# An encoder layer in split fp32: seven-product projection pairs ahead of the mixers, and new fill between the mixers' steps

## The chip, the cores and the metric

The kernel runs on one core of one Trainium2 chip. The metric is the device time of one execution in microseconds (us). Engines are named as the profile names them: PE is the matrix engine, DVE, ACT and POOL work on vectors, and SP issues transfers. Line numbers such as L633 are those of the kernel before, unless the text says that they are of the kernel after.

## The reference

One layer of a bidirectional encoder on x, 1024 tokens by 1024 features, in fp32:

```python
u = x @ W_in                            # rq, rk, rv, rg (512 each), aq (512), ak, av (128 each)
y_ret = retention(rq, rk / 8, rv)       # 8 heads of 64, forward and backward, chunks of 128
y_ret = groupnorm(y_ret) * silu(rg)
y_att = windowed_attention(aq, ak, av)  # 8 query heads, 2 key heads, +-128 tokens, sink logit
h = LN1(ALPHA * x + concat(y_ret, y_att) @ W_out)
f = (silu(h @ W_g) * (h @ W_u)) @ W_d + sigmoid(h @ W_pg) * (p @ W_pe)
out = LN2(ALPHA * h + f)                # ALPHA = 2 ** 0.25, W_g and W_u are 1024 x 2816
```

## The kernel before

**Arithmetic.** Every fp32 operand of a large matmul is split into a high and a low part (`split`, L73 on ACT for the high part and L74 on DVE for the low one). One product of two such operands is three PE matmuls (`mm3`, L77 to L79): high by high, high by low, low by high. Each has a stationary block of 128x128 and 512 moving columns. In this text "a product" is such a triple and "a matmul" is one of its three.

**Stages in order.**

1. *First f-tiles* (L132 to L180). A column tile of 128 features of `u` is an f-tile. Four f-tiles (the first attention query tile, ak, rk of pair 0, rq of pair 0) are accumulated in all eight banks of PSUM while x streams in. The split x stays in four buffers named H.
2. *Mixers* (up to L600). Four pairs of heads, each with a retention (`Retention`) and an attention (`Attention`). Their steps are short matmuls with DVE, ACT and POOL work between them, so the program interleaves them with *fill*: steps of one product of the rest of the input projection, taken from `queue`. PE's order is written out by hand here (`manual_schedule` for PE); the other engines' orders come from a scheduler. `run(steps, total)` spreads `total` fill steps evenly over the places marked `F`. The fill is 288 steps: 14 f-tiles of 16 steps, and rv, which `proj_rv` makes in token-major form in 64 steps. Attention 0 runs in 16 + 64 of them, retention 0 in 48, then three iterations (retention i with attention i) in 48 each, and 16 remain for the end. In the names below, K is `keys` (transposes of rk at L363, times a decay on DVE at L366), C is `kv` (L377 on PE, L381 on DVE), Q is the scores of the retention, Y its output, N its norm, and X the transposes that turn the normed result (L455 on PE, L456 on ACT).
3. *Output projection* (L568 to L690). The eight mixer results are split (yT) and multiplied by w_out: 384 matmuls. Tokens come in eight tiles of 128 (t = 0 to 7), each in two halves of 512 columns. Phase 1 does t = 0 to 3 for all eight k-tiles in eight banks (192 matmuls); phase 2 does t = 4 to 7 one after another (48 matmuls each), and in each the program puts `ln1_apply` and `to_hT` of tile t - 4. For each half, DVE adds ALPHA * x to the bank (`zpart`, L629) and takes statistics (L633); `ln_rstd` is L637 and L638 on DVE and a power on POOL (L639); `ln1_apply` is two DVE operations of 1024 columns (L644, L645); `to_hT` is eight transposes on PE (L660), two copies on ACT (L661), two DVE subtractions (L662) and a scaling on ACT (L663).
4. *Embedding gate* (`ple`, up to L760). Four groups of 96 matmuls (h @ W_pg), with the transposes of t = 4 to 7 and some sums for the next stage as side steps. After each group, for four token tiles: 6 matmuls of p @ W_pe, the sigmoid on ACT (L758), and a multiplication and an addition on DVE (L759, L760). The buffer `sg` of the sigmoid is double.
5. *Feed-forward*: gate and up in pairs of f-tiles by a seven-product scheme (two-by-two blocks with sums of blocks, seven block products in place of eight; L826 to L828), results to DRAM, then down in the same scheme. DVE, ACT, POOL and SP have hand-written orders here too.

Stages 3 and 4 are ordered by a scheduler on every engine.

## Time and profile before

| | us |
|---|---|
| median of 3 runs | 1225.3 (1224.57 to 1226.44) |
| the profiled execution | 1223.15 |
| span of its trace | 1221.4 |
| first f-tiles | 0 to 49.4 |
| mixers, first part (attention 0, retention 0) | 49.4 to 170 |
| mixers, three iterations and the remaining fill | 170 to 377.4 |
| output projection, phase 1 and phase 2 | 377.4 to 421 and 421 to 468.5 |
| embedding gate | 468.5 to 575 |
| feed-forward | 575 to 1221.4 |

How to read the profile's rows. A row by stretches gives the stretch, its length, then for each engine busy time and instructions, the granted PE clock (1.00 is full speed), the share of busy DMA engines and GB/s. A row of the timeline gives start, duration, engine, line, operation, output and inputs with their shapes, the count of instructions joined in it, and in brackets how long the engine had been idle and what ended that. A row of a group gives its count, busy time, the mean duration of one in ns, and the idle time before them. A row of waits gives who waited for whom, the sum, the count and the longest. PE overlaps matmuls, so one that lasts 0.39 us by its record can still be followed by the next after 0.23 us; costs on PE are counted from start to start.

### The profile page before, as it was taken

The page shows a single profiled execution, that of the slowest core. Times are in us where ns is not written, and L with a number is a line of the kernel's source. Part 1 is how long each engine was busy: PE and PEld are TensorE (multiplying, and loading weights), DVE is VectorE, ACT ScalarE, POOL GpSimd, SP SyncE. Part 2 cuts the span into 40 slices and gives each one's busy share as a digit, 9 for nine tenths or more (in the row PEclk, how much of TensorE's full clock was granted, in tenths as well). Part 3 has the DMA queues.
Part 4 walks back from the last instruction along what each step waited for, and adds up shares of the span by engine and source line. Part 5 has one row for each costly group of instructions (what it writes and reads, how often), then busy time and mean ns, then how long its engine had stood idle before and what let it go on. Part 6 is the DMA issues. An engine that isn't in the chain of part 4 may idle for free.

```text
span 1221.4 us, 16350 instructions
## 1 busy us (share of the span) xinstructions
PE 1208.0 (99%) x5987; PEld 999.1 (82%) x5987; DVE 723.0 (59%) x1282; ACT 467.7 (38%) x867; POOL 375.6 (31%) x347
## 2 busy tenths in 40 slices
PE   9999999999999999999999999999999999999997
PEld 7888878888888888888888888888888888888885
DVE  5542566676755486793755554555545555875668
ACT  5643124444665024432433332333233334652452
POOL 2000011112010020000575646557465523034236
PEclk9999999999999999999999999999999999999999
DMA  6310010100104313032332223322233149999977
GB/s 250 91 45 1 18 35 19 35 18 19 36 19 151 111 45 121 18 106 102 142 129 81 91 89 129 130 83 91 86 129 130 70 150 284 389 268 215 261 182 207
DMA packets 56688, 139.63 MB, mean 114 GB/s; under 512 B 6816, under 2 KB 8992, under 8 KB 56608
## 3 DMA queue, kind: packets, MB, share of 16 engines
q1 hardware_dynamic: 47968, 121.81, 28.3%
q0 software_dynamic: 8640, 16.78, 7.9%
q8 instruction: 47, 0.77, 0.3%
q14 instruction: 33, 0.27, 0.1%
HBM read 104.75 MB, written 28.57 MB: 109 GB/s over the span
## 4 chain that ended last, share of the span: by engine, by line
PE 91%; DVE 5%; issue 1%; ACT 1%; DMA 1%; POOL 1%; DVEq 0%; ACTq 0%; SPq 0%; POOLq 0%
PE bmm L77 7%; PE bmm L78 7%; PE bmm L79 7%; PE bmm L828 4%; PE bmm L826 4%; PE bmm L827 4%; PE bs L826 4%; PE bs L828 4%; PE bs L827 4%; PE bo L826 4%; PE bo L827 4%; PE bo L828 4%; PE bt L826 4%; PE bt L828 4%; PE bt L827 4%; PE bs L79 2%
## 5 line engine op out<-in xcount | busy, mean ns | idle before, releaser
L77 PE MATMUL bmm<-H,w 128*128 128x512 f32 x240 | 100.7, 420 | 0.9 <-DVE rkq L218 0.9
L79 PE MATMUL bmm<-H,w 128*128 128x512 f32 x240 | 94.4, 393 | 0.0
L78 PE MATMUL bmm<-H,w 128*128 128x512 f32 x240 | 94.2, 393 | 0.0
L74 DVE TENSOR_TENSOR w<-raw,w 128x512 fp32r<-128x512 f32 x80 | 60.4, 765 | 52.7 <-ACT w L73 52.4
L863 POOL TENSOR_TENSOR H<-ln 128x512 f32<-128x512 f32 x22 | 28.4, 1293 | 192.9 <-PE bo L79 111.9
L893 POOL TENSOR_TENSOR ev<-ev 128x512 f32<-128x512 f32 x33 | 54.9, 1664 | 91.4 <-DVE ev L908 38.6
L481 POOL COPY sc<-skb 128x1 f32<-128x1 f32 x64 | 17.0, 275 | 203.1 <-PE bt L502 154.3
L74 DVE TENSOR_TENSOR w<-H,w 128x512 fp32r<-128x512 f32 x44 | 40.8, 927 | 63.9 <-ACT w L73 63.9
L73 ACT ACTIVATE w<-raw 128x512 fp32r<-128x512 f32 x80 | 48.9, 625 | 61.6 <-PE bmm L79 29.6
L897 POOL TENSOR_TENSOR ev<-ev,ev 128x512 f32<-128x512 f32 x44 | 62.7, 1437 | 2.6
L891 ACT ACTIVATE ev<-ev 128x512 f32<-128x512 f32 x33 | 20.9, 632 | 102.3 <-DVE ev L908 102.3
L74 DVE TENSOR_TENSOR u<-H,u 128x512 fp32r<-128x512 f32 x47 | 36.2, 769 | 40.0 <-ACT u L73 39.6
L490 ACT ACTIVATE sc<-sc,st 128x385 f32<-128x385 f32 (+1 forms) x64 | 37.2, 583 | 46.2 <-DVE st L488 46.2
L486 DVE CUSTOM_DVE_ANT_0 sc<-cst,bs,skb 128x384 f32<-128x384 f32 (+1 forms) x64 | 35.1, 576 | 32.9 <-PE bs L485 32.9
L77 PEld LDWEIGHTS bmm<-H,w 128*128 128x128 f32 x240 | 45.3, 189 | 11.2 <-DVE rkq L218 2.2
L79 PEld LDWEIGHTS bmm<-H,w 128*128 128x128 f32 x240 | 45.2, 188 | 10.2
L78 PEld LDWEIGHTS bmm<-H,w 128*128 128x128 f32 x240 | 45.4, 189 | 6.2
L73 ACT ACTIVATE u<-H 128x512 fp32r<-128x512 f32 x47 | 29.6, 630 | 43.2 <-PE bmm L828 9.0
L639 POOL TENSOR_TENSOR stt<-stt,cst 128x1 f32<-128x1 f32 x8 | 11.6, 1455 | 99.6 <-DVE stt L638 99.6
L448 POOL TENSOR_TENSOR sm<-sm,cst 128x8 f32<-128x8 f32 x8 | 13.9, 1737 | 78.4 <-DVE sm L447 78.4
L867 POOL TENSOR_TENSOR H<-raw,H 128x512 f32<-128x512 f32 x22 | 37.8, 1717 | 0.0
L73 ACT ACTIVATE w<-H 128x512 fp32r<-128x512 f32 x44 | 27.4, 622 | 24.4 <-PE bmm L828 6.3
(642 smaller groups left out, 3717.6 us busy)
## 6 DMA issues: line engine op xcount, KB each, us to landing
ad<-ev SPq DMA_DIRECT2D x33, 512.0 KB, 2.6
raw<-in_w_gu SPq DMA_DIRECT2D x22, 512.0 KB, 4.3
ln<-in_w_gu SPq DMA_DIRECT2D x22, 512.0 KB, 3.5
raw<-ad SPq DMA_DIRECT2D x40, 256.0 KB, 6.0
ln<-ad SPq DMA_DIRECT2D x37, 256.0 KB, 6.5
H<-in_w_dn SPq DMA_DIRECT2D x33, 256.0 KB, 6.3
raw<-in_w_mt SPq DMA_DIRECT2D x14, 512.0 KB, 3.5
h0b<-in_w_dn POOLq DMA_DIRECT2D x24, 256.0 KB, 6.9
```

Source lines behind the costliest of these rows:

```text
L73: act.activation(hi, raw, AF.Copy)
L74: dve.tensor_tensor(lo, raw, hi.bitcast(F32), ALU.subtract)
L77: pe.matmul(o, lh, rh, start=start, stop=False)
L78: pe.matmul(o, lh, rl, start=False, stop=False)
L79: pe.matmul(o, ll, rh, start=False, stop=stop)
L490: act.activation(sc[g][:, :nk + 1], sc[g][:, :nk + 1], AF.Exp, bias=st_[:, 1, j, g:g + 1], accum_out=st_[:, 2, j, g:g + 1])
L826: pe.matmul(o, lh, rh, start=start, stop=False, skip_group_check=True)
L827: pe.matmul(o, lh, rl, start=False, stop=False, skip_group_check=True)
L828: pe.matmul(o, ll, rh, start=False, stop=stop, skip_group_check=True)
L867: pool.tensor_tensor(s[3], a(0, 1), s[0], ALU.subtract)
L893: pool.tensor_tensor(c[:, 1, :], c[:, 0, :], c[:, 1, :], ALU.mult)
L897: pool.tensor_tensor(self.ev[dst][:, 0, :], left, right, op)
```

## The change

- **Projection.** Twelve f-tiles (rk, rq and query tile of pair 1, rk and rq of pair 2, all four rv tiles, the gates of pairs 2 and 3, and av) become six pairs (`Proj`) that run right after the first f-tiles, by the same seven-product scheme as the feed-forward, 84 matmuls for a pair in place of 96. All five engines have a hand-written order in this stage. Sums of blocks of x are made by `x_sums` and `x_put`. The results go to DRAM (`ud`) and are read back by `load_pair` and `rv_load` during the iteration before their use; av, rv of pair 0 and the first f-tiles stay in SBUF.
- **rv** is now made feature-major, so each iteration turns it with eight more PE transposes (`turned`, line 447 after, copied by ACT at line 448 after) ahead of C(0). The query tiles are scaled from SBUF by `conv_q` (four operations of 64x1024 on ACT and DVE) rather than from PSUM halves (`ev_aq`); the scale of rk moves into the masks and the decay.
- **Mixers.** There are four like iterations with 48, 48, 48 and 36 fill steps, and the rest follows. The fill is four f-tiles that are still made singly (query tiles of pairs 2 and 3, rk and rq of pair 3), the gates of pairs 0 and 1, p @ W_pe in two parts (`embedding`, to DRAM), and half of the output projection (`half_out`: the first four k-tiles, to which ALPHA * x is added, to DRAM as z0): 192 steps. `half_out`'s load (four splits of mixer results and eight of w_out) is called at the first step of `embedding(1)`.
- **Output projection.** Phase 1 and phase 2 take only k-tiles 4 to 7 (96 + 96 matmuls); z0 is loaded into the accumulator and `zpart` adds the bank to it. LN1 and `to_hT` are as before (lines 820 to 850 after).
- **Embedding gate.** No p @ W_pe here: its result is loaded from DRAM, and the multiplication by the sigmoid moves from DVE to POOL (line 916 after).

The core of the diff:

```diff
+    class Proj:                       # one pair of f-tiles, seven products
+        def prep(self, p):
+            if not self.raw:
+                self.load()
+            if p not in (1, 2) and not self.s:
+                self.sums()
+            src = self.s[p] if p in self.s else self.raw[{1: (0, 0), 2: (0, 1), 4: (1, 1)}[p]]
+            t = self.ops[p] = op_tile()
+            split(src, t[:, 0, :], t[:, 1, :])
+        def mm(self, p):
...
+            for kt in range(4):
+                c = slice(kt * P, (kt + 1) * P)
+                rh, rl = right(p, kt)
+                mm3c(b, w[:, 0, c], w[:, 1, c], rh, rl, first and kt == 0, kt == 3)
...
+        for k, (pr, p) in enumerate(punits):
+            pr.mm(p)
+            pr.post(p, k)
+            pahead(k + 1 + min(7, 4 + k))
...
+    def turned(src, dst):
+        def half(h):
+            tb = bank("t", (P, 4, P))
+            for j in range(4):
+                n = 4 * h + j
+                pe.transpose(tb[:, j, :], src[:, n * P:(n + 1) * P], ident)
+            act.activation(dst[:, 4 * h:4 * h + 4, :], tb, AF.Copy)
+        return half
...
+        rvs[i] = bt([P, NT, P], "rv", 1)
...
+    def half_out():
+        def load():
+            for k in range(4):
+                turn_y(k)
+            for kt in range(4):
+                if kt % 2 == 0:
+                    wb = big16((P, 2, 2, 2, HF))
+                out_weights(kt, [wb[:, kt % 2, j] for j in range(2)])
+        def step(t, h, kt):
+            if kt == 0:
+                hold["b"] = bank("mm")
+                hold["x"] = wp.tile([P, 2, HF], F32, tag="w", bufs=4, name=nm("w"))[:, 0, :]
+                sp.dma_start(hold["x"], xn[t, h])
+            outp(hold["b"], t, h, kt, 0, 3)
+            if kt == 3:
+                dve.scalar_tensor_tensor(x, x, ALPHA, hold["b"], ALU.mult, ALU.add)
+                sp.dma_start(z0[t][:, hs[h]], x)
...
-            run([K(0), Q(0), F, X0, F, C(0), F, X1, K(1), F, C(1), sco(0), F,
+            run([K(0), Q(0), F, X0, F, (turn_rv, 0), C(0), F, X1, (turn_rv, 1), gat, K(1), F, C(1), sco(0), F,
...
-                Y(1, 1), N(1), trn(6), F, trn(7), F, F, val(6), val(7)], 48)
-        run([F, X(0), F, X(1), F, F], 16)
+                val(4), val(5), F, Y(1, 1), N(1), trn(6), F, trn(7), F, F, val(6), val(7)], 48 if i < 3 else 36)
+        run([F, X(0), F, X(1), F, F], 100)
...
-        dve.scalar_tensor_tensor(accs[t][:, h * HF:(h + 1) * HF], xr[h], ALPHA, b, ALU.mult, ALU.add)
+        dve.tensor_tensor(z, z, b, ALU.add)
...
-    for kt in range(KT):
+    for kt in range(4, KT):
         for t in range(4):
             for h in range(2):
-                outp(bs[t, h], t, h, kt)
+                outp(bs[t, h], t, h, kt, 4, KT - 1)
...
-            if kt == 3:
+            if kt == 5:
                 ln1_apply(t - 4)
                 to_hT(t - 4)
...
-            dve.tensor_tensor(sg, sg, b2, ALU.mult)
+            pool.tensor_tensor(sg, sg, e, ALU.mult)
             dve.tensor_tensor(accs[t][:, sl], accs[t][:, sl], sg, ALU.add)
```

PE's order where an iteration begins, before (retention 2's first steps; `ym` is the normed result of the pair before, `H` the split x, `rv` and `kdec` the operands of C(0)):

```order
L455 MATMUL bt_2113<-cst,ym_1771 128x128 x4
L77 MATMUL bmm_2109<-H_95,w_1874 128x512
L78 MATMUL bmm_2109<-H_95,w_1874 128x512
L79 MATMUL bmm_2109<-H_95,w_1874 128x512
L77 MATMUL bmm_2109<-H_164,w_1874 128x512
L78 MATMUL bmm_2109<-H_164,w_1874 128x512
L79 MATMUL bmm_2109<-H_164,w_1874 128x512
L377 MATMUL bt_2125<-rv_432,kdec_2082 128x128 x3
```

And after (line 447 turns rv, `raw` is rv read back from DRAM, line 512 is C(0)):

```order
L447 MATMUL bt_2109<-cst,raw_1927 128x128 x4
L512 MATMUL bt_2115<-rv_1929,kdec_2066 128x128 x3
L83 MATMUL bmm_2093<-H_188,w_1795 128x512
L84 MATMUL bmm_2093<-H_188,w_1795 128x512
L85 MATMUL bmm_2093<-H_188,w_1795 128x512
L83 MATMUL bmm_2093<-H_255,w_1798 128x512
L84 MATMUL bmm_2093<-H_255,w_1798 128x512
L85 MATMUL bmm_2093<-H_255,w_1798 128x512
L590 MATMUL bt_2127<-cst,ym_1959 128x128 x4
L447 MATMUL bt_2133<-cst,raw_1927 128x128 x4
L498 MATMUL bt_2139<-cst,rkq_1760 128x128 x2
```

Before, C(0) reads an rv that was finished long ahead. After, the first half of rv is turned in the four transposes just ahead of C(0), with no fill between them, and C(0) reads the copy that ACT makes of them.

DVE's order in iteration 2, at the first steps of `embedding(1)` after (`A` is a mixer result, `raw` a part of w_out, `pr` a tile of p, `st` and `sc` belong to attention; L80 after is the low part of a split):

```order
L80 TENSOR_TENSOR H_2982<-A_2045,H_2982 128x1024
L80 TENSOR_TENSOR H_2987<-raw_2988,H_2987 128x512 x2
L80 TENSOR_TENSOR H_2987<-raw_2994,H_2987 128x512 x2
L623 TENSOR_SCALAR st_2838<-st_2838 128x2
L80 TENSOR_TENSOR p_3086<-pr_3084,p_3086 128x256
L80 TENSOR_TENSOR p_3122<-pr_3120,p_3122 128x256
L627 RECIPROCAL st_2838<-st_2838 128x2
L629 TENSOR_SCALAR sc_3040<-sc_3040,st_2838 128x384
L629 TENSOR_SCALAR sc_3041<-sc_3041,st_2838 128x384
L80 TENSOR_TENSOR H_3000<-raw_3001,H_3000 128x512 x2
L80 TENSOR_TENSOR H_3000<-raw_3007,H_3000 128x512 x2
L80 TENSOR_TENSOR p_3156<-pr_3154,p_3156 128x256
```

Before, DVE at the corresponding place of its iteration (a scan of the retention, attention's rows, and one split of a weight tile):

```order
L392 SCALAR_TENSOR_TENSOR kv_2717<-kv_2717,cd 128x128
L494 TENSOR_SCALAR sc_2904<-sc_2904,st_2813 128x384
L494 TENSOR_SCALAR sc_2905<-sc_2905,st_2813 128x384
L392 SCALAR_TENSOR_TENSOR kv_2717<-kv_2717,cd 128x128 x3
L551 TENSOR_TENSOR y_1052<-y_1052,sq_2949 128x512
L392 SCALAR_TENSOR_TENSOR kv_2717<-kv_2717,cd 128x128
L74 TENSOR_TENSOR w_2957<-raw_2952,w_2957 128x512
```

After, splits of mixer results and of w_out stand among attention's short operations and ahead of the splits of p that the next fill steps read; before, a weight tile's splits stood there one at a time.

PE's order where the output projection gives way to the embedding gate, before (`acc` is a normed token tile, L660 its transposes, L77 to L79 the gate's matmuls on `h0a`):

```order
L77 MATMUL bs_4155<-w_4125,h0a_3763 128x512
L78 MATMUL bs_4155<-w_4125,h0a_3763 128x512
L79 MATMUL bs_4155<-w_4125,h0a_3763 128x512
L660 MATMUL bt_4180<-cst,acc_3765 128x128 x4
L660 MATMUL bo_4187<-cst,acc_3765 128x128 x4
L77 MATMUL bmm_4152<-w_4130,h0a_3763 128x512
```

After (line 847 has the transposes, of token tiles 3, 4 and 5 in turn):

```order
L83 MATMUL bmm_4656<-w_4626,h0a_4388 128x512
L83 MATMUL bs_4658<-w_4626,h0a_4388 128x512
L83 MATMUL bmm_4657<-w_4626,h0a_4388 128x512
L847 MATMUL bt_4571<-cst,acc_4381 128x128 x4
L847 MATMUL bo_4578<-cst,acc_4381 128x128 x4
L83 MATMUL bs_4659<-w_4626,h0a_4388 128x512
L847 MATMUL bt_4684<-cst,acc_4390 128x128 x4
L847 MATMUL bo_4691<-cst,acc_4390 128x128 x4
L847 MATMUL bt_4723<-cst,acc_4443 128x128 x4
L847 MATMUL bo_4730<-cst,acc_4443 128x128 x4
L84 MATMUL bmm_4656<-w_4626,h0a_4388 128x512
```

Before, the transposes of token tile 4 stood behind 24 matmuls of the gate and those of tile 5 behind 48. After, those of tiles 3, 4 and 5 stand within the gate's first four matmuls.

More of the change, by code (lines that the diff above doesn't have):

```diff
@@ L114, in big16 @@
         return big.tile(list(shape), F32R, tag="H", bufs=4, name=nm("H"))
-    bp = cstack.enter_context(contextlib.ExitStack())
-    bpool = bp.enter_context(tc.tile_pool(name="bp", bufs=1))
-    def bt(shape, tag, bufs=None, dt=F32):
-        return bpool.tile(list(shape), dt, tag=tag, bufs=bufs, name=nm(tag))
-    zero = bt([P, HF], "sq", 1, mybir.dt.bfloat16)
-    pool.memset(zero, 0.0)
-    zb = bank("o")
-    for _ in range(WARM):
-        pe.matmul(zb, zero[:, :P], zero, start=True, stop=True)
@@ new lines, in tt, with atile @@
+    def tt(shape, tag, bufs=None, dt=F32):
+        return tpool.tile(list(shape), dt, tag=tag, bufs=bufs, name=nm(tag))
+    hs = [slice(h * HF, (h + 1) * HF) for h in range(2)]
+    def atile(shape=(P, S), dt=F32):
+        return big.tile(list(shape), dt, tag="A", bufs=8, name=nm("A"))
+    A = [atile() for _ in range(8)]
+    xs, st, wf = [], {}, []
+    cst = cp.tile([P, C_W], F32, name="cst")
+    masks = cp.tile([P, 2, P], mybir.dt.bfloat16, name="masks")
+    ident = cst[:, C_ID:C_ID + P]
@@ new lines, in layer, with pahead @@
+    punits = [(pr, p) for n, pr in enumerate(projs) for p in ((1, 6, 5, 2, 7, 4, 3) if n else (1, 2, 6, 5, 7, 4, 3))]
+    pdone = [0]
+    def pahead(upto):
+        while pdone[0] < min(upto, len(punits)):
+            pr, p = punits[pdone[0]]
+            pr.prep(p)
+            pdone[0] += 1
+    ET = mybir.EngineType
+    with tc.manual_schedule(engines={ET.PE, ET.DVE, ET.Activation, ET.Pool, ET.SP}):
+        zero = tt([P, HF], "s1", 2, mybir.dt.bfloat16)
+        pool.memset(zero, 0.0)
+        zb = bank("o")
+        for _ in range(WARM):
+            pe.matmul(zb, zero[:, :P], zero, start=True, stop=True)
+        for (m, h), t in zip([(m, h) for m in range(4) for h in range(2)], [t for t in ("mm", "s", "t", "o") for _ in range(NB[t])]):
+            st[m, h] = bank(t)
@@ L207, in layer @@
-    cd = cp.tile([P, 8], F32, name="cd")
-    act.activation(cd, lg[:, 16:24], AF.Exp, scale=float(P))
+                    xt[:, 0, hs[h]], xt[:, 1, hs[h]], kt == 0, kt == KT - 1)
+            if kt > 4:
+                x_put(kt - 5)
+            if kt >= 4:
+                x_sums(kt - 4)
+        pahead(2)
+        consts_in()
+        first = [atile() for _ in range(4)]
+        for m in range(4):
+            t = first[m]
+            act.activation(t[:, hs[0]], st[m, 0], AF.Copy)
+            dve.tensor_copy(t[:, hs[1]], st[m, 1])
@@ new lines, in layer @@
+        x_put(3)
+        pahead(4)
+        for k, (pr, p) in enumerate(punits):
+            pr.mm(p)
+            pr.post(p, k)
+            pahead(k + 1 + min(7, 4 + k))
+            while late and late[0][0] <= k:
+                late.pop(0)[1]()
+            if k == 8:
+                tables()
+        for _, f in late:
+            f()
+    tstack.close()
+    bp = cstack.enter_context(contextlib.ExitStack())
+    bpool = bp.enter_context(tc.tile_pool(name="bp", bufs=1, reuse_waits="tile"))
@@ L211, in slope, with bt, conv_q @@
+    def bt(shape, tag, bufs=None, dt=F32):
+        return bpool.tile(list(shape), dt, tag=tag, bufs=bufs, name=nm(tag))
     def slope(i, g):
         return 2.0 ** -(i + 4 * g + 1)
-    def ev_rk(b, rk, h):
-        act.activation(rk[:, h * HF:(h + 1) * HF], b, AF.Copy, scale=0.125)
-    def ev_rq(b, rq, h):
-        dve.tensor_copy(rq[:, h * HF:(h + 1) * HF], b)
-    def ev_aq(b, qs, h, i):
-        sl = slice(h * HF, (h + 1) * HF)
+    def conv_q(i, raw):
+        qs = [bt([P, S], "aq", 3, F32R) for _ in range(2)]
@@ new lines, in layer, with turn_y, out_weights, outp @@
+    yT, wo = [], {}
+    def turn_y(k):
+        if len(yT) % 2 == 0:
+            turn_y.p = big16()
+        t = turn_y.p[:, :, len(yT) % 2, :]
+        split(ys[k], t[:, 0, :], t[:, 1, :])
+        yT.append(t)
+    def out_weights(kt, tiles):
+        r = rawt(2 * HF)
+        sp.dma_start(r, w_out[kt])
+        for j in range(2):
+            split(r[:, hs[j]], tiles[j][:, 0, :], tiles[j][:, 1, :])
+        wo[kt] = tiles
+    def outp(b, t, h, kt, first, stop):
+        c = slice(t * P, (t + 1) * P)
+        w = wo[kt][h]
+        mm3(b, yT[kt][:, 0, c], yT[kt][:, 1, c], w[:, 0, :], w[:, 1, :], kt == first, kt == stop)
```

457 lines of the change are left out of this document (244 added, 213 removed).

## The prediction

> **What bounds the kernel now.** I read the page first: busy shares, slices, clock, and the chain of work that ended last.
>
> ```profile
> span 1221.4 us, 16350 instructions
> PE 1208.0 (99%) x5987; PEld 999.1 (82%) x5987; DVE 723.0 (59%) x1282; ACT 467.7 (38%) x867; POOL 375.6 (31%) x347
> PE   9999999999999999999999999999999999999997
> PEclk9999999999999999999999999999999999999999
> PE 91%; DVE 5%; issue 1%; ACT 1%; DMA 1%; POOL 1%; DVEq 0%; ACTq 0%; SPq 0%; POOLq 0%
> ```
>
> PE is busy in every slice, at full clock, and is 91% of the chain. So matmuls removed are time saved, one for one, and every new wait of PE is time lost, one for one. The question is how many waits the new order makes. For that I read the stretches that the change rebuilds.
>
> ```profile
> core 0: us, PE busy (x) PEld busy (x) DVE busy (x) ACT busy (x) POOL busy (x), PEclk, DMA share, GB/s
> 300.40:377.40 77.00, 76.36 (x506) 64.54 (x505) 47.26 (x128) 49.29 (x91) 8.32 (x18) 1.00 0.16 52
> 377.40:421.00 43.60, 43.37 (x191) 35.59 (x191) 20.31 (x29) 12.50 (x21) 0.00 (x0) 1.00 0.31 99
> 421.00:468.50 47.50, 47.50 (x227) 39.62 (x227) 39.62 (x62) 11.31 (x16) 10.06 (x7) 1.00 0.28 89
> 468.50:575.00 106.50, 105.95 (x476) 85.41 (x475) 72.76 (x99) 39.95 (x63) 1.52 (x1) 1.00 0.25 85
> 575.00:1003.00 428.00, 428.00 (x1888) 353.72 (x1887) 226.13 (x287) 135.55 (x230) 239.40 (x161) 1.00 0.30 108
> ```
>
> The row that matters most is 421 to 468.5, phase 2 of the output projection: DVE works 39.62 of 47.5 us there (83%), against 59% over the span. It is hidden because phase 1 left it half idle (20.31 of 43.6) and phase 2 is long. The waits of PE by the waits view are small:
>
> ```profile
> PE bo L129 <- POOL sq L126: 1.3, 1, 1.3
> PE bmm L77 <- DVE rkq L218: 0.9, 3, 0.4
> PE bt L377 <- DVE kdec L366: 0.6, 1, 0.6
> PE bt L502 <- ACT sc L490: 0.5, 1, 0.5
> ```
>
> After the start no listed wait lasts as long as 1 us.
>
> **Removed and added PE work.** The price of a matmul is 428.0 / 1888 = 0.227 us, from the feed-forward row, where PE is never idle and runs the very scheme that the change adds. Twelve f-tiles in six pairs, each 96 - 84 = 12 matmuls cheaper, are 72 matmuls: -16.3 us. Each of four iterations turns rv by eight transposes.
>
> ```profile
> 302.79 0.44 PE bt L455 x4
> ```
>
> 32 transposes at 0.44 per four are +3.5 us. The 96 matmuls of p @ W_pe and 192 of the output projection only change place. Net **-12.8 us**.
>
> **The new projection stage** is the feed-forward's pattern with hand-written orders: DVE is 226/428 = 53% busy there and POOL 56%, so I cost its waits at 0 (-1 to +3, since x sums and the decay tables also pass through DVE and POOL).
>
> **The start of the mixers** moves behind that stage. The buffers of the mixers take over the space of the stage's operands, so the conversion of the first query tile and of the keys starts only when its last matmuls are done: six ACT copies and four DVE operations of 64x1024.
>
> ```profile
> L227 DVE SCALAR_TENSOR_TENSOR aq<-bmm,aq 64x512 fp32r<-64x512 f32 x8 | 5.5, 688 | 3.6 <-ACT aq L226 3.5
> 373.56 4.86 ACT L73 ACTIVATE H<-y 128x1024 fp32r<-128x1024 f32 x5 [0.66 <-PE bmm L79]
> 311.35 1.28 ACT L550 ACT_TABLE_LOAD   x1 [3.50 <-PE bmm L79]
> ```
>
> A copy of 1024 columns is 4.86 / 5 = 0.97 us, so ACT has 5.8 us queued plus a table load of 1.28, and the turns of av and rv stand behind them on ACT while PE has only a few fill steps of 0.68 us to offer. I count 5 us of waits, against some 2.5 us around the first steps now (the 0.9 and 0.6 above among them): **+2.5** (1 to 5).
>
> **Turning rv ahead of C(0).** The transposes are followed at once by C(0), which reads ACT's copy, so PE waits for one copy of 512 columns and the path to it.
>
> ```profile
> L456 ACT ACTIVATE y<-bt,gn 128x512 f32<-128x512 f32 x5 | 3.4, 689 | 6.7 <-PE bt L455 6.7
> L366 DVE TENSOR_TENSOR kdec<-bt,kd 128x256 f32<-128x256 f32 x16 | 6.0, 419 | 0.9 <-PE bt L363 0.7
> ```
>
> 0.69 us for ACT's copy and some tenths on the way, in three further iterations (the first is counted above), and with one rv buffer the turn also waits for the last reader: 1.0 each, **+3** (1 to 5).
>
> **Iteration 2** receives half_out's load: four splits of 1024 columns and eight of 512 on ACT and on DVE, ahead of the splits of p that the next fill steps read.
>
> ```profile
> 374.65 4.63 DVE L74 TENSOR_TENSOR H<-y,H 128x1024 fp32r<-128x1024 f32 x4 [1.60 <-ACT H L73]
> 416.94 0.69 DVE L629 SCALAR_TENSOR_TENSOR acc<-raw,bmm 128x512 f32<-128x512 f32 x1 [15.06 <-PE bmm L79]
> 417.62 0.69 DVE L629 SCALAR_TENSOR_TENSOR acc<-raw,bs 128x512 f32<-128x512 f32 x1
> 419.42 0.67 DVE L629 SCALAR_TENSOR_TENSOR acc<-raw,bt 128x512 f32<-128x512 f32 x1
> ```
>
> DVE takes 4.63 / 4 = 1.16 for each of the large ones, and for one of 512 columns 0.60 from start to start (four of them from 416.94 to 419.42, two of these the statistics): 4 x 1.16 + 8 x 0.60 = 9.4 us of extra DVE work, as much on ACT, in an order in which attention's reciprocals and the splits of p stand behind them. A fill step that reads p gives 1.36 us per token tile (six matmuls). Walking the order with these prices gives waits of 4.3 and 1.5 us; if the load drifts ahead of them, none. I take **+4** (0 to 8).
>
> **Iteration 3** has 36 fill steps instead of 48: 36 matmuls or 8.2 us less cover for the same attention chain. In the row for 300 to 377 DVE is only 61% busy, so most of it is slack; **+2** (0 to 7).
>
> **Mixers to output projection.** The last half_out matmuls read split results that must be freed before the splits for k-tiles 4 to 7 can be made (0.97 on ACT, then 1.16 on DVE), and the buffers for two parts of w_out wait for stores of z0.
>
> ```profile
> ad<-ev SPq DMA_DIRECT2D x33, 512.0 KB, 2.6
> ```
>
> A store of twice that size lands in 2.6 us. Copy, subtraction and one store's tail make 3.5 us where the trace now has 0.5: **+3** (1 to 5).
>
> **The output projection.** Let E be the end of phase 1. Phase 2 shrinks to 96 matmuls (21.8 us), and phase 1 likewise, but DVE's work behind E does not shrink: `zpart` is now a DVE addition of the same shape.
>
> ```profile
> 426.56 0.34 DVE L637 BATCH_NORM_AGGREGATE stt<-stt 128x2 f32<-128x12 f32 x3
> 426.86 1.27 DVE L644 SCALAR_TENSOR_TENSOR acc<-acc,stt,ln 128x1024 f32<-128x1024 f32 x1
> 428.05 0.15 DVE L638 TENSOR_SCALAR stt<-stt 128x1 f32<-128x1 f32 x1
> 429.31 2.48 DVE L645 SCALAR_TENSOR_TENSOR acc<-acc,stt,ln 128x1024 f32<-128x1024 f32 x2
> 432.95 0.69 DVE L662 TENSOR_TENSOR h0a<-bt,h0a 128x512 fp32r<-128x512 f32 x1
> 433.55 0.69 DVE L662 TENSOR_TENSOR h0b<-bo,h0b 128x512 fp32r<-128x512 f32 x1
> L639 POOL TENSOR_TENSOR stt<-stt,cst 128x1 f32<-128x1 f32 x8 | 11.6, 1455 | 99.6 <-DVE stt L638 99.6
> ```
>
> From 416.94 to 426.56 DVE needs 9.6 us for the 16 operations of t = 0 to 3; they can start some 4.5 us before E, when the first bank is complete, and end at E + 5.1. Then every further tile costs 2.4 (two additions, two statistics), every LN1 0.3 + 1.19 + 1.19 = 2.7, every `to_hT` 1.2, and POOL's power of 1.46 is exposed now and then. Before the transposes of tile 5 can start, DVE has done two more tiles (4.8), six LN1 (16.2) and five low parts (6.0): E + 32.1, and with the exposed power and ACT's copies E + 33 to E + 38. PE arrives there after 100 matmuls (22.7 us) and five times eight transposes (4.4): E + 27.1. Step by step I find waits of 2.7, 4.5 and 3.0 us ahead of tiles 3, 4 and 5, and 1.1 for the low part of the first gate weight, queued on DVE behind them: 11.3, where phase 2 and its end have some 2.3 today. The order after puts the transposes of tiles 4 and 5 within the gate's first four matmuls; before, they stood 24 and 48 matmuls later, so nothing else covers them. **+9** (6 to 12). This is the term I trust most.
>
> **The gate.** Without p @ W_pe (24 matmuls per group) only the next group covers the chain sigmoid, POOL multiplication, DVE addition through two buffers.
>
> ```profile
> 492.32 1.28 ACT L758 ACTIVATE sg<-bmm 128x512 f32<-128x512 f32 x2 [0.52 <-PE bmm L79]
> L897 POOL TENSOR_TENSOR ev<-ev,ev 128x512 f32<-128x512 f32 x44 | 62.7, 1437 | 2.6
> ```
>
> Two tiles in flight cost 0.6 + 1.44 + 0.6 before a buffer is free, about 2.6 us for the third tile's bank; the next group starts on the first banks, which are free. **+0.5** (0 to 4).
>
> **Sum.** Waits: 0 + 2.5 + 3 + 4 + 2 + 3 + 9 + 0.5 = +24.0; with -12.8 that is +11.2 us. The profiled execution, 1223.15 (its span 1221.4 plus 1.75 around it), becomes 1234.4. It lies 2.1 us below the median of the runs shown, so on the median, 1225.3, the forecast is **1236.5**.
>
> **Rivals.**
> *The walls are soft (the other side).* In-order walks overstate waits when each engine has drifted ahead. The mechanism has its place in the output stage: if the DVE chain above reached tile 5 by E + 27 (it would need to start 10 us earlier, or banks to be freed earlier than phase 1 suggests), and the mixers' splits ran ahead, only the start's +2.5 and some tenths would stay: 1225.3 - 12.8 + 2.5 = 1215. It decides when all waits together stay below 10.4 us. For it: no wait above 1.3 us in the whole trace of before, and DVE only 59% busy. Against it: the 83% row. Chance 0.15.
> *Only the hard walls bind.* Output stage +9 and the boundary +3, with iterations as smooth as now: -12.8 + 12 = -0.8, 1224.5, no change. For it: the iterations' DVE shares of about 61%. Chance 0.13.
> *The clock falls.* Waits of 3 to 4.5 us could cost the full clock.
>
> ```profile
> 1.31 3.17 PE bo L129 x7
> ```
>
> At the cold start seven matmuls take 3.17 us, 0.45 each, twice the price of 0.227. A wait that brings this back costs half of such a stretch, 1.6 us, once or twice in the output stage: 1238 to 1240. The trace of before has no gap that could show whether a wait of this length does it, and its PEclk row is all nines. The Trainium skill, "TensorE: Matmul & The Clock Gate", in "Why this matters for your kernels", advises against idle gaps of PE above about 3 us in a kernel, because the clock then falls back to half. By that rule the waits of 4.5 and 3.0 us would each bring the half rate back and the time would be this rival's. The trace agrees on the half rate at the start; on gaps it is silent. Chance 0.12.
>
> **How the numbers follow.** The forecast's own case has 0.60. Slower is 0.60 + 0.12 = 0.72, same 0.13, faster 0.15; a difference of 0.2% (2.45 us) is about what a measurement of this kernel can tell from no change. Adding the terms' lower spreads in squares (1, 1.5, 2, 4, 2, 2, 3, 0.5) gives 6 us and the upper ones (3, 2.5, 2, 4, 5, 2, 3, 3.5) 9: 1230 to 1246. The clock extends the top to 1248; to leave out no more than 2 in 10, the bottom reaches the no-change rival and a little past it, 1222.
>
> **What would show each step.** 72 fewer matmuls of 512 columns and 32 more transposes; the projection stage without PE waits above 0.5 us; PE waiting for ACT's rv copy (line 448 after) about 1 us in each iteration; a PE wait of some us for a split of p in iteration 2; and, the main point, PE idle some 10 us in all ahead of the transposes at line 847, released by DVE's LN1 (line 832), with DVE near 100% from E to then. If those last waits are absent or under 4 us in sum, the forecast is wrong; if PEclk shows less than 1.00 there, the third rival holds.

## The result

The changed kernel takes 1269.6 us (median of 4 runs, 1267.7 to 1272.5), the kernel before 1224.9 in the same comparison: ratio 1.0366, 95% interval 1.0339 to 1.0392. It is slower by 45 us, where 11 were forecast, and lies above the stated range.

The page of the changed kernel, its busy row, two rows of slices and the chain:

```profile
span 1270.7 us, 16667 instructions
PE 1214.5 (96%) x5947; PEld 1000.0 (79%) x5947; DVE 781.3 (61%) x1335; ACT 501.2 (39%) x924; POOL 448.4 (35%) x395
PE   9979999999989999798899999999999999999996
PEclk9988999999989999799999999999999999999999
PE 75%; DVE 9%; issue 6%; POOL 4%; ACT 3%; DMA 3%; SPq 0%; DVEq 0%; POOLq 0%; ACTq 0%
```

PE's share of the chain fell from 91 to 75%. The rows of slices say where: PE is lower in slices 3, 12, 17, 19 and 20 (of 31.8 us each), and in slices 3, 4, 12 and 17 the granted clock is below full as well. PE has 5987 - 5947 = 40 instructions fewer, which is 72 matmuls removed and 32 transposes added, as counted.

PE's waits, the largest first (who waits, for whom, sum, count, longest):

```profile
PE bs L83 <- ACT sg L915: 7.2, 4, 3.5
PE bt L279 <- DVE A L260: 5.5, 2, 4.8
PE bmm L85 <- DVE p L80: 5.4, 3, 3.9
PE bs L279 <- DVE A L260: 5.1, 1, 5.1
PE bt L847 <- DVE stt L825: 4.0, 1, 4.0
PE bt L512 <- ACT rv L448: 3.5, 4, 1.5
PE bt L847 <- DVE acc L832: 2.6, 2, 1.8
```

L915 is the gate's sigmoid, L260 a post of the projection stage, L80 the low part of a split (here of p), L825 and L832 are LN1, L448 is the copy of rv. The rows for rv, p and LN1 were forecast, those for the gate and the projection stage were not. Now the stretches (the columns are as before):

```profile
44.00:178.50 134.50, 121.40 (x506) 97.92 (x506) 62.38 (x88) 42.20 (x73) 43.91 (x34) 0.95 0.27 90
316.00:385.00 69.00, 61.93 (x401) 51.52 (x401) 49.90 (x130) 47.42 (x97) 11.88 (x22) 0.95 0.33 111
484.00:515.00 31.00, 31.00 (x151) 25.72 (x149) 28.64 (x50) 8.33 (x13) 2.72 (x4) 1.00 0.28 111
515.00:530.00 15.00, 7.13 (x29) 5.19 (x28) 14.38 (x23) 4.97 (x9) 4.77 (x5) 0.60 0.00 1
570.00:626.00 56.00, 48.57 (x196) 38.25 (x195) 39.63 (x38) 15.28 (x22) 18.63 (x12) 0.94 0.38 132
```

In order: the projection stage, iteration 2, the output projection, its end (DVE works 14.38 of 15 us while PE works 7.13), and the last half of the embedding gate. To put sums beside the prediction's terms I took the start of every PE instruction from both traces and subtracted its price: 0.227 us for 512 columns, and for a shorter shape its mean from start to start in the trace of before, gaps over 0.26 us left out. What remains is waits and half-rate matmuls; a stage begins with its first PE instruction.

| stage | before | after | more | forecast |
|---|---|---|---|---|
| price of all PE work | 1186.8 | 1173.8 | -13.0 | -12.8 |
| first f-tiles | 2.6 | 2.6 | 0 | 0 |
| projection stage | | 20.2 | +20.2 | 0 |
| mixers | 17.5 | 35.3 | +17.8 | +11.5 |
| output projection and gate | 4.3 | 26.8 | +22.5 | +12.5 |
| feed-forward | 0.6 | 2.7 | +2.1 | 0 |

The sum is +49.6 us, the difference of the two spans is 49.3. That is more than the 45 of the medians because the profiled execution, 1272.5 us, is the slowest of the four; the feed-forward's +2.1 is one wait of 2.2 us at 1246 us, which no trace of e1 to e9 has. The rest asks why the rows of the projection stage, of the mixers and of output projection and gate are so large.

### The profile page after: what moved, and what is told of

Its sections match the earlier page's. It is cut to its first block, busy times and chain, and to the rows that moved or that the text cites. A ratio compares the mean times of both kernels' runs of the same rounds, so it can differ in the third digit from the quotient of the medians.

```text
span 1270.7 us, 16667 instructions
## 1 busy us (share of the span) xinstructions
PE 1214.5 (96%) x5947; PEld 1000.0 (79%) x5947; DVE 781.3 (61%) x1335; ACT 501.2 (39%) x924; POOL 448.4 (35%) x395
## 4 chain that ended last, share of the span: by engine, by line
PE 75%; DVE 9%; issue 6%; POOL 4%; ACT 3%; DMA 3%; SPq 0%; DVEq 0%; POOLq 0%; ACTq 0%
PE bmm L279 5%; PE bmm L281 5%; PE bmm L280 5%; PE bs L279 4%; PE bs L281 4%; PE bs L280 4%; PE bt L279 4%; PE bt L280 4%; PE bt L281 4%; PE bo L280 4%; PE bo L279 4%; PE bo L281 4%; PE bmm L83 3%; PE bmm L85 3%; PE bmm L84 3%
## 5 line engine op out<-in xcount | busy, mean ns | idle before, releaser
L80 DVE TENSOR_TENSOR w<-raw,w 128x512 fp32r<-128x512 f32 x72 | 56.8, 800 | 67.3 <-ACT w L79 67.2
L616 POOL COPY sc<-skb 128x1 f32<-128x1 f32 x64 | 19.8, 319 | 188.0 <-PE bt L637 146.4
L80 DVE TENSOR_TENSOR w<-H,w 128x512 fp32r<-128x512 f32 x44 | 37.6, 854 | 62.1 <-ACT w L79 62.1
L79 ACT ACTIVATE w<-raw 128x512 fp32r<-128x512 f32 x72 | 44.1, 624 | 57.9 <-DMA raw<-in_w_pg 17.4
L80 DVE TENSOR_TENSOR u<-H,u 128x512 fp32r<-128x512 f32 x47 | 35.2, 748 | 39.1 <-ACT u L79 38.7
L80 DVE TENSOR_TENSOR u<-raw,u 128x512 fp32r<-128x512 f32 x36 | 39.1, 1089 | 15.9 <-ACT u L79 15.9
L83 PE MATMUL bmm<-H,w 128*128 128x512 f32 x112 | 47.8, 426 | 0.0
L916 POOL TENSOR_TENSOR sg<-sg,pe 128x512 f32<-128x512 f32 x16 | 24.8, 1567 | 60.7 <-ACT sg L915 40.5
L79 ACT ACTIVATE u<-H 128x512 fp32r<-128x512 f32 x47 | 29.6, 630 | 41.6 <-PE bs L281 11.1
L84 PE MATMUL bmm<-H,w 128*128 128x512 f32 x112 | 44.3, 396 | 0.0
L85 PE MATMUL bmm<-H,w 128*128 128x512 f32 x112 | 44.2, 394 | 0.0
L79 ACT ACTIVATE u<-raw 128x512 fp32r<-128x512 f32 x36 | 22.6, 629 | 35.3 <-PE bt L281 8.0
L79 ACT ACTIVATE w<-H 128x512 fp32r<-128x512 f32 x44 | 27.4, 622 | 22.7 <-PE bs L281 8.3
L1009 POOL TENSOR_TENSOR H<-H,raw 128x512 f32<-128x512 f32 x22 | 35.4, 1607 | 1.7
L639 ACT ACTIVATE ptr<-bt 128x384 f32<-128x384 f32 (+1 forms) x64 | 26.2, 456 | 18.7 <-PE bt L637 18.6
```

What stands on the lines that cost most here:

```text
L79: act.activation(hi, raw, AF.Copy)
L80: dve.tensor_tensor(lo, raw, hi.bitcast(F32), ALU.subtract)
L83: pe.matmul(o, lh, rh, start=start, stop=False)
L84: pe.matmul(o, lh, rl, start=False, stop=False)
L85: pe.matmul(o, ll, rh, start=False, stop=stop)
```

## The experiments

The runs e1 to e9 are the changed kernel with one place altered (three in e5), one run each. Single times differ by some us without a cause in the edit: the four of the changed kernel lie between 1267.7 and 1272.5, and the first f-tiles alone took 47.7 to 50.1 us. So I read the stage's excess over price, as in the table, beside the time (1269.6 for the changed kernel). Where the edit lies elsewhere, that excess came out within about 1.5 us for the projection stage (18.8 to 20.2), within about 1 us for output projection and gate and, but for e5, for the mixers.

**The projection stage.** The first long wait in the trace of the changed kernel: DVE, POOL and PE in their timelines.

```profile
59.29 0.69 DVE L80 TENSOR_TENSOR w<-raw,w 128x512 fp32r<-128x512 f32 x1
64.73 2.76 DVE L80 TENSOR_TENSOR u<-ss,u 128x512 fp32r<-128x512 f32 x2 [4.76 <-ACT u L79]
67.42 0.68 DVE L80 TENSOR_TENSOR u<-raw,u 128x512 fp32r<-128x512 f32 x1
68.02 0.68 DVE L260 TENSOR_TENSOR A<-s,bt 128x512 f32<-128x512 f32 x1
```

```profile
61.38 1.29 POOL L221 TENSOR_TENSOR ss<-raw 128x512 f32<-128x512 f32 x1 [9.23 <-DMA raw<-in_w_mt]
```

```profile
68.84 0.77 PE L279 MATMUL bt<-T,w 128*128 128x512 f32 x1 [4.75 <-DVE A L260]
69.41 0.63 PE L280 MATMUL bt<-T,w 128*128 128x512 f32 x1
69.83 0.63 PE L281 MATMUL bt<-T,w 128*128 128x512 f32 x1
```

PE needs the post at L260, which reads a bank that the next unit adds to. The post takes 0.68 us but stands on DVE behind splits of the next pair's sums, which wait for ACT, for POOL, and in the end for a load of weights that could start only when the pair before had given up its two raw buffers. Behind the wait, matmuls follow each other after 0.42 us instead of 0.227: half rate. The second wait, in the same trace:

```profile
86.28 4.17 POOL L159 TENSOR_TENSOR lt<-cst,rr 128x24 f32<-128x24 f32 x1
```

```profile
90.49 0.18 DVE L160 TENSOR_SCALAR lt<-lt 128x24 f32<-128x24 f32 x1 [5.67 <-POOL lt L159]
95.05 0.68 DVE L260 TENSOR_TENSOR A<-s,bs 128x512 f32<-128x512 f32 x1
```

POOL's power for the decay tables, 4.17 us, holds DVE up for 5.67 us, and another post at L260 comes after it.

*e2_tables* (`powers` is the mask copy and POOL's power, taken out of `tables`):

```diff
+            if k == 0:
+                powers()
```

> The changed kernel with one edit: POOL's power for the decay tables (4.17 us) and the mask copy are issued after the first projection unit, ahead of the second pair's sums, and not after the ninth unit behind the third pair's. Theory (DVE and ACT, in order, stood behind that power, and a post that frees PE's bank behind them): the 5.1 us wait near 90 us and the 12 half-rate matmuls behind it go, about 6.5 us; 1263. Rival (the post waits for the splits of the next pair's sums, not for the tables): the wait stays at 3 us or more. Second rival: the power now delays the second pair's sums, and the earlier wait near 64 us grows by what the later one loses.

1262.2 us; the stage's excess 20.2 became 12.9. The wait near 90 us fell to 0.94, the one near 64 stayed at 5.05. The theory holds, both rivals fall.

*e3_look*:

```diff
-            pahead(k + 1 + min(7, 4 + k))
+            pahead(k + 1 + (4, 4, 4, 3, 4, 5, 6)[k] if k < 7 else k + 8)
```

> The changed kernel with one edit: the operands of the second pair's sums are prepared fewer units ahead at the start (so that the post of unit 4 stands ahead of them in DVE's order). Theory (DVE waits in order for sums that wait for the weights' load, with the post that frees PE's bank behind): the 4.8 us wait near 64 us shrinks to about 1 us and its half-rate stretch goes, 5 to 6 us; 1264. Rival (the load itself is late, and whoever reads it makes PE wait a unit later): less than 2 us come back, the wait only moves to the second pair's unit.

1264.9 us; excess 16.0. The first wait fell from 4.9 to 1.03 us, but the second grew:

```profile
PE bs L279 <- DVE A L260: 8.2, 1, 8.2
```

With the engines ahead of the first wait, PE reaches the tables sooner and waits longer there. What came back, some 4 us, lies between the theory and its rival: the causes stand in series, so an edit to the first gives back only what the second does not take.

*e5_proj*, both, and the order of units:

```diff
-    ... for p in ((1, 6, 5, 2, 7, 4, 3) if n else (1, 2, 6, 5, 7, 4, 3))]
+    ... for p in ((1, 6, 5, 7, 2, 4, 3) if n else (1, 2, 6, 5, 7, 4, 3))]
```

> The changed kernel with three edits in the projection stage together: the powers for the tables early, the shorter lookahead at the start, and units of a pair in the order 1, 6, 5, 7, 2, 4, 3, so that no unit accumulates into a bank right behind the unit whose post reads it. Theory (the stage's 20 us over the matmuls' price are three separate causes, in-order waits behind the tables, behind the second pair's sums, and 0.94 us at every pair for unit 4 behind unit 7, each long wait with a half-rate stretch): the stage's waits fall to about 2 us in all, 1269.6 becomes about 1251. Rival (the stage is bound by the weights' loads or by POOL's sums, and what is taken from one wait goes to the next, as the lookahead alone did with 3 us of its gain): 1256 or more, with a wait over 3 us left.

1259.6 us; excess 6.4, 14 back where 18 were expected. By its time, and by the one long wait that is left, this run shows the rival's signs and not the theory's; the mixers' excess is 2 us higher in it. The 0.94 us waits at each pair went, which shows the third cause; one wait of 3.7 us was left (the tables' ACT and DVE steps and the third pair's sums, again ahead of a post). In e10 below the tables' steps are also issued three units earlier and the lookahead is held down for the second pair too: excess 2.4. That settles the stage: the same work on the same engines waits 2.4 us when it is issued in another order, so its 20 us are in-order queues, not PE work and not a lack of engine time.

**The gate.** ACT, POOL and PE at the third group, changed kernel:

```profile
581.53 1.20 ACT L915 ACTIVATE sg<-bs 128x512 f32<-128x512 f32 x2 [1.90 <-DVE acc L917]
```

```profile
576.33 4.55 POOL L916 TENSOR_TENSOR sg<-sg,pe 128x512 f32<-128x512 f32 x2 [16.64 <-DVE w L80]
```

```profile
582.18 0.50 PE L83 MATMUL bs<-w,h 128*128 128x512 f32 x1 [3.54 <-ACT sg L915]
...
583.42 0.63 PE L84 MATMUL bs<-w,h 128*128 128x512 f32 x1
583.85 0.63 PE L85 MATMUL bs<-w,h 128*128 128x512 f32 x1
```

Two multiplications take POOL 4.55 us; until DVE has added the product, both sigmoid buffers are taken, the third and fourth sigmoids wait, and with them the two banks that the next group needs. The 4.55 us are not two equal halves. All sixteen multiplications and all sixteen additions (shortest, median and longest in ns):

```profile
L916 POOL TENSOR_TENSOR sg<-sg,pe x16: 1260/1292/3335, 551.4 to 637.4; 128x512 f32<-128x512 f32 x16
L917 DVE TENSOR_TENSOR acc<-acc,sg x16: 673/1213/1773, 552.8 to 638.7; 128x512 f32<-128x512 f32 x16
```

The first of the two took 3.33 us, with DVE at work on its sums and splits, the second 1.26, and DVE's addition behind the first took 1.74 us. The last section says when each is long.

*e1_banks*:

```diff
-        bg = [bank(("mm", "s")[k // 2]) for k in range(4)]
+        bg = [bank((("mm", "s"), ("t", "o"))[(len(turns) - 1) % 2][k // 2]) for k in range(4)]
```

> The changed kernel with one edit: the four groups of the embedding gate take turns between two sets of four banks, so a group's first matmuls no longer wait for the sigmoids of the group before. Theory (the lost cover of p @ W_pe let PE wait for the sigmoids, and the clock fell behind each such wait): the two waits of 3.5 and 2.7 us and the half-rate stretches behind them go; the stretch from the output projection's end to the feed-forward gets 9 to 12 us shorter, 1269.6 becomes about 1259. Rival (DVE's sums or the gate weights' loads are late there anyway, the sigmoid is only the last of several): at most 4 us come back, and another releaser stands at the same place.

1268.5 us. The waits on the sigmoid went, and this came:

```profile
PE bmm L279 <- ACT ev L1062: 6.0, 1, 6.0
PE bmm L84 <- DVE w L80: 2.9, 1, 2.9
```

The rival holds in size but not in place: excess of the gate 25.7 to 16.2, but that of the feed-forward 2.7 to 8.2, whose first evacuation (L1062) stands on ACT behind the last group's sigmoids. Other banks only move the wait; the chain is what is slow.

*e8_sgdve*:

```diff
-            pool.tensor_tensor(sg, sg, e, ALU.mult)
+            dve.tensor_tensor(sg, sg, e, ALU.mult)
```

> The changed kernel with the gate's multiplication back on DVE instead of POOL. Theory (the wait of a group's banks is the chain sigmoid, multiplication, addition through two buffers, and POOL's 1.4 to 2.3 us, with the feed-forward's sums in its queue, is the long link): the waits on the sigmoid fall from 7.2 us to 3 or 4, and the clock holds: 4 to 7 us, about 1264. Rival (the chain waits for the load of p @ W_pe's result from DRAM, or DVE, in order behind its sums, is late itself): no more than 2 us.

1260.1 us; excess 25.7 to 14.7, and the waits on the sigmoid above 0.75 us are gone. More than expected: with the multiplication on DVE the gate's loss of 11 us is gone, though p @ W_pe's matmuls are still missing. Whether POOL would have cost anything with those matmuls in place was not run.

**The output projection.** *e4_outm*:

```diff
-    ... for t in range(NT) for h in range(2) for kt in range(4)]      # half_out
+    ... for t in range(4) for h in range(2) for kt in range(4)]
-    ... 48 if i < 3 else 36)
+    ... 40 if i < 3 else 32)
-        for kt in range(4, KT):                                        # phase 2
+        for kt in range(KT):
```

> The changed kernel with half of the output projection moved into the mixers for token tiles 0 to 3 only; tiles 4 to 7 take all eight k-tiles in phase 2, as before the change, and the mixers' fill is 160 steps (40, 40, 40, 32 and 8) for 192. Same number of matmuls. Theory (phase 2 had become too short to hide DVE's additions, statistics and LN1): the waits ahead of the transposes of tiles 3, 4 and 5 (11 us with the clock) fall to under 2, and the mixers lose at most 4 us for the thinner fill: 1269.6 becomes 1260 to 1264. Rival (the iterations need 48 steps to hide the attention's chain, which is why the fill was put there): the iterations lose 8 us or more and the time stays at 1266 or rises.

1261.6 us. Of output projection and gate the excess fell from 26.8 to 13.6, so the waits on LN1 with their half rate had been 13 us; no wait on LN1 is left. The mixers' excess rose from 35.3 to 38.8, over 96 matmuls less of fill:

```profile
PE bt L512 <- ACT rv L448: 5.1, 4, 3.0
PE bmm L83 <- ACT p L79: 2.6, 1, 2.6
```

The theory holds in kind and size.

**The mixers.** *e6_rvearly*:

```diff
-            run([K(0), Q(0), F, X0, F, (turn_rv, 0), C(0), F, X1, (turn_rv, 1), gat, K(1), F, C(1), sco(0), F,
+            run([K(0), (turn_rv, 0), Q(0), F, X0, (turn_rv, 1), F, C(0), F, X1, gat, K(1), F, C(1), sco(0), F,
```

> The changed kernel with rv's transposes a few steps earlier in each iteration (first half behind the first keys step, second half behind the transposes of the normed result), so that fill and scores stand between them and C(0). Theory (PE waits for ACT's copy of the transposes because C(0) follows at once): the waits on ACT's rv copy, 3.5 us in four, fall below 1 us; 2 to 4 us, about 1266. Rival (rv read back from DRAM or its single buffer is late as well): the wait moves to the transposes, no gain.

1266.0 us; the mixers' excess 35.3 to 30.9. The theory holds: 4.4 us.

*e7_spread*:

```diff
-        return [load], ...
+        loads = [lambda k=k: turn_y(k) for k in range(4)] + [lambda kt=kt: weights(kt) for kt in range(4)]
+        return loads, ...
```

> The changed kernel with the load of the half output projection spread: its four splits of mixer results and four pairs of splits of w_out go to eight places in the last embedding tile's 16 steps, where they all stood at the first. Theory (splits of p stand in order behind them on DVE and ACT): the 3.9 us wait and the 1.4 us one in iteration 2 and the half-rate stretch go, 5 to 7 us, about 1264. Rival (DVE and ACT are full there, so the same work only makes other steps wait, in iteration 3 or at the first half_out steps): under 2 us.

1274.6 us, worse; excess 38.2. The wait for p moved 20 us on and stayed at 3.6. The rival holds.

*e9_poolw*, in `out_weights`, for half_out's splits:

```diff
-            split(r[:, hs[j]], tiles[j][:, 0, :], tiles[j][:, 1, :])
+            act.activation(tiles[j][:, 0, :], r[:, hs[j]], AF.Copy)
+            pool.tensor_tensor(tiles[j][:, 1, :], r[:, hs[j]], tiles[j][:, 0, :].bitcast(F32), ALU.subtract)
```

> The changed kernel with the low parts of the eight w_out splits of half_out on POOL instead of DVE (POOL is under 20% busy in the iterations). Theory (in iteration 2 the splits of p stand in order behind 4.8 us of these on DVE): the 3.9 us wait falls to about 2 (the four splits of mixer results still stand ahead) and its half-rate stretch goes, 3 to 5 us, about 1265. Rival (the operands are late on ACT, which makes the high parts and loads its tables, so DVE's share does not decide; or the H buffers come free late): under 1.5 us.

1272.2 us; excess 39.5. The wait on DVE's splits of p fell to 2.6, and ACT took its place:

```profile
PE bmm L83 <- ACT p L79: 7.0, 2, 6.1
```

My theory that DVE's share decides there falls. POOL and ACT in that run:

```profile
351.99 6.18 POOL L723 TENSOR_TENSOR H<-raw,H 128x512 fp32r<-128x512 f32 x4 [4.89 <-ACT H L722]
```

```profile
362.32 1.15 ACT L722 ACTIVATE H<-raw 128x512 fp32r<-128x512 f32 x2 [1.67 <-DMA raw<-in_w_out]
...
365.79 0.72 ACT L79 ACTIVATE p<-pr 128x256 fp32r<-128x256 f32 x2
```

POOL holds the two raw buffers for 6.18 us, the next loads come late, ACT stands at the splits that read them, and p's split comes after those.

**Combinations.** *e10_combA* (two runs, 1238.7 and 1244.4) has the repaired projection stage, the multiplication on DVE and rv early; *e11_combB* adds the edit of e4; *e12_combC* adds that of e9; *e14_pre* is e11 with p's tiles split two tiles ahead.

> The changed kernel with the edits that each took a wait away: powers and tables early, lookahead kept below the posts for the first two pairs, units in the order 1, 6, 5, 7, 2, 4, 3; the gate's multiplication on DVE; rv's transposes early. The output projection stays as changed. Theory (causes add up): the projection stage's waits fall to 2 to 3 us (18 back), the gate gives 9.5 and rv 3: 1269.6 - 30 = about 1239. Rival (waits move on to the next late engine): 1247 or more. Against the kernel before it is still slower, by the output projection's 9 to 11 us and iteration 2's 8.

1241.6 us (ratio 1.0124, 1.0072 to 1.0175): the causes add up, 28 of the 30 us expected came back.

> The same edits as in the run with the output projection as changed, and on top the output projection of token tiles 4 to 7 kept whole in phase 2 (40, 40, 40, 32 and 8 fill steps). Theory: another 8 us back, and rv's early transposes spare the mixers part of what the thin fill cost: 1228 to 1232, within 0.6% of before. Rival (the thin fill's loss grows when the other waits, which gave the engines time, are gone): 1236 or more.

1228.8 us (1.0039, 1.0019 to 1.0059), as the theory had it.

> The previous combination with the low parts of half_out's w_out splits on POOL. Theory (the last large wait in the mixers is the splits of p behind half_out's load): 3 us less than without, about 1226. Rival: ACT or the H buffers decide there, no difference.

1232.8 us (1.0056, 1.0038 to 1.0074): no gain, and its longest wait is 6.9 us, again on ACT's split of p.

> The combination with half_out for token tiles 0 to 3, and p's tiles loaded and split two tiles ahead, so that two of the splits stand ahead of half_out's load in ACT's and DVE's order. Theory (it is only the place in the order that makes PE wait): the 2.8 and 1.5 us waits go, 1224 to 1226. Rival (ACT and DVE have too much to do in that stretch, or the buffers for raw weights are held too long there): the wait comes two tiles later, 1227 to 1230.

1230.0 us (1.0054, 1.0035 to 1.0074). The waits for p fell below 1 us, and the next in line, 3.0 us in e11, grew:

```profile
PE bt L451 <- DMA raw<-ud: 5.2, 1, 5.2
```

rv of the next pair is read back into the same raw buffers that half_out's weights occupy. After three edits that each moved it, the wait in iteration 2 is explained by half_out's load as a whole (splits on two engines and two raw buffers), not by one place in an order.

*e13_nohalf* takes that load away: no half_out, five pairs instead of six, gates of pairs 2 and 3 as fill, output projection as before the change.

```diff
-        ..., ((RGI[2], "silu"), (RGI[3], "silu")), ...
-        enqueue([spill(AQI[2]), spill(RKI[3]), embedding(0), spill(RQI[3]), spill(AQI[3]), gate(0), gate(1), embedding(1),
-                 half_out()])
+        enqueue([spill(AQI[2]), spill(RKI[3]), embedding(0), spill(RQI[3]), spill(AQI[3]), embedding(1), gate(0), gate(1),
+                 gate(2), gate(3)])
```

> The repaired kernel (tables, lookahead and unit order of the projection stage, gate's multiplication on DVE, rv's transposes early) without the half output projection: five seven-product pairs, the gates of pairs 2 and 3 made in the mixers as before the change, p @ W_pe as fill, the output projection whole behind the mixers as before the change; 36 fill steps in each iteration and 16 behind. 12 more matmuls than the changed kernel, +2.7 us. Theory (half_out's load of splits into iteration 2 and the short phase 2 cost more than they cover): against the combination with half_out for four token tiles, the waits of 2.8, 1.5 and 3.1 us with their half-rate matmuls go (8 to 10 us) for 2.7, and 36 steps in place of 40 cost 1 to 3: 1221 to 1226, no slower than the kernel before. Rival (the thin fill is what makes the engines late there): 1229 or more, with waits inside the iterations.

1224.5 us (ratio 1.0004, 0.9994 to 1.0013), even with the kernel before: its PE work is priced 10.3 us lower, its excess is 36.5 against 25.1. It differs by more than the load, so it does not single the load out. Its largest wait:

```profile
PE bt L450 <- DVE kdec L504: 3.0, 1, 3.0
```

The decay of the first keys stands on DVE behind the conversion of the query tile and the attention's keys, at the start of the mixers.

*e15_best* issues that conversion behind the first keys step, with the turns of av and rv and the scores moved around it, and splits p two tiles ahead:

```diff
+                [K(0), F, (turn_rv, 0), F, Q(0), (first_keys,), F, (turn_rv, 1), C(0), F, X0, K(1), F, X1, C(1), F, sco(0), F]
```

> The version without the half output projection, with two edits more: at the start of the mixers the first keys step stands ahead of the conversion of the first query tile and of the attention's keys (in DVE's and ACT's order, too), and p's tiles are split two tiles ahead. Theory (the 3.1 and 1.4 us waits at 151 and 157 us are kdec behind four conversions on DVE, the 1.4 and 1.6 us waits are late splits of p; the rest of its 35 us over the matmuls' price is spread): 4 to 6 us back, 1218 to 1221, faster than the kernel before by 0.3 to 0.5%. Rival (the attention's first scores, which now get their operands later, wait instead): 1223 to 1226, no difference.

1222.1 us, ratio 0.998 (0.997 to 0.9989): faster than the kernel before by 0.2%, less than the theory's lower end. The waits for p are gone, but at the start of the mixers the wait only changed its name, which neither theory had foreseen:

```profile
PE bt L455 <- ACT rv L456: 2.7, 1, 2.7
```

ACT's copy of rv now stands behind what was moved.

## Why the prediction was wrong

**The price of PE work** (-12.8) was right: -13.0 by the traces.

**The projection stage** is the step that failed most: "the feed-forward's pattern with hand-written orders ... so I cost its waits at 0 (-1 to +3, ...)". It cost 20.2. I compared engine shares, but by the code the feed-forward works on two halves in turn, so each post has another unit's matmuls as cover and a pair is 14 units; here one pair is one chain of 7 (0.94 us at every pair, e5), its operands are prepared seven units, that is a whole pair, ahead in the same DVE queue as the posts (e3), and only two raw buffers feed it. The tables, which the text did mention, were put down as part of +3; they alone were some 7 us (e2).

**The gate** (+0.5, 0 to 4) failed too: 11.0 by e8. The step was "the next group starts on the first banks, which are free". The first two are; the other two wait for the sigmoid buffers, so for POOL's multiplication and DVE's addition: 3.33 and 1.74 us at that place where I took 1.44 and 0.6.

**The output projection** (+9, 6 to 12) had the right mechanism, place and rows of the order. The excess there, from 498 to 532 us, is 13.0, which e4 took away; before, from 421 to 500 us, it was 2.0, as the text said, so the term came to +11. PE's waits alone were 1.4 at the last tile's bank and 1.1, 4.6 and 2.1 ahead of tiles 3, 4 and 5, in all 9.2 where the walk had 11.3; the other 3.8 are half rate, which had been put into a rival.

**The mixers** (+11.5): the sum was 17.8. rv's turns 4.4 for 3 (e6); iteration 2 some 7 for 4, by the trace's excess from 350 to 375 us, with the mechanism forecast but in size nearer its upper bound; the start some 5 for 2.5, by the excess from 175 to 200 us; iteration 3, with 36 steps, showed next to nothing of its +2 (its excess is 6.1 us, but 4.6 in e6, where rv is turned early, and 4.0 in an iteration before).

**Mixers to output projection** (+3): the trace has 0.6 us there. The stores of z0 were done in time.

**The rivals.** The clock's (0.12) came true, together with the forecast's mechanism and not instead of it, and it was priced at 1.6 us once or twice. Five waits of 3.5 to 5.2 us (64, 90, 352, 519 and 578 us) and a pair of 2.9 and 0.9 (605) were each followed by matmuls at half rate (at 519 the clock was at half already, from 518.1 on). Matmuls of 512 columns that followed the last one after 0.33 to 0.5 us cost 14.3 us over their price, against 6.3 before; that is 8 us of the 49 between the traces. The page of the Trainium skill that I cited, "TensorE: Matmul & The Clock Gate", warns in "Why this matters for your kernels" of gaps above about 3 us: the changed kernel's trace agrees. In it waits of 0.7 to 2.3 us standing alone were followed by at most three slower matmuls, those at 64 and 90 us by 12 each. Over all runs the length of the gap does not decide, and there the measurement differs from that section: in e10 a wait of 2.0 us and in e14 one of 2.2 were followed by five, and in e5 one of 3.8 us, at 86 us, was not followed by half rate. The last section shows what does fit.

"The walls are soft" fell: only the boundary behind the mixers and iteration 3 were softer than priced. "Only the hard walls bind" fell with the mixers' +17.8.

## What to carry to other kernels

In a queue that works in order, price an operation by what stands ahead of it, not by its engine's share: here a post of 0.7 us that PE needed stood behind splits that waited for another engine or a load, at 5 us a time. When work that covered a chain is taken away (half an output projection over LN1) or a link of it changes engines (the gate's multiplication), walk the chain again with its buffers and with what the other engines do in that stretch. Count a wait that leaves PE less than half busy for a few us as longer than it is: those of 4.9 and 5.2 us at 64 and 90 us cost some 2.8 us more in half-rate matmuls. And a repaired wait can move: e1, e7 and e9 only moved theirs, and e3 gave part of its gain to the next.

## What the runs showed of the hardware that was not expected

**The clock goes by intervals of 3.41 us.** How much half rate follows a wait varies: after the same wait of 4.05 us in iteration 2 the clock was at half for 3.41 us in e2 and e8 and for 10.24 us in e5. In each of the 17 traces the granted clock changes only at multiples of 3.41 us from its first change. One such interval in the changed kernel, with the first half of the wait at 352 us in it, and the two behind it together:

```profile
350.85:354.26 3.41, 1.41 (x16) 0.81 (x12) 3.41 (x8) 3.41 (x6) 0.00 (x0) 1.00 0.17 66
354.26:361.09 6.83, 4.93 (x19) 4.45 (x20) 4.33 (x11) 4.60 (x10) 0.67 (x2) 0.50 0.70 232
```

And the wait of 3.8 us in e5, which falls into two intervals and leaves PE 46% busy in each:

```profile
84.27:87.68 3.41, 1.58 (x7) 0.96 (x6) 2.65 (x9) 2.27 (x7) 1.09 (x1) 1.00 0.00 0
87.68:91.10 3.42, 1.59 (x7) 1.32 (x8) 2.94 (x6) 2.50 (x5) 0.00 (x0) 1.00 0.00 0
```

Between the cold start and the last 12 us the traces have 60 intervals at full clock in which PE, by its records, was busy 45% or less; each was followed by one at half clock. Of some 5900 with more than 50% none was; between the two, 8 of 15. So what decides in these runs is how a wait falls on the intervals, not its length alone. This is read from the traces; no edit was made to test it. The cold start goes with it: the first f-tiles ended at 48.9 to 49.5 us where the full clock came 4.1 to 6.6 us into the span, and at 50.6 to 51.4 where it came at 9.2 to 10.5.

**POOL and DVE held each other up.** Of the gate's sixteen multiplications on POOL the five that began while DVE had 0.4 us or more of an operation on SBUF tiles left took 1.61 to 3.33 us, the other eleven 1.26 to 1.30. Eight of DVE's additions, which read two SBUF tiles, began while POOL was in a multiplication or a sum and took 1.73 to 1.77 us; the other eight took 0.67 to 0.69. In the feed-forward before, 45 additions of DVE that read one of their inputs from PSUM began within an operation of POOL and took no longer than the rest, 0.67 to 0.69 us. There is no exception among these rows, but no edit was made to test the cause. The row that the prediction took for POOL, 1.44 us, is a mean over multiplications of 1.3 and of 1.6 to 1.75.
